# Layer 0's branch and output turned by VectorE's 32x32 block transposes and a trip through memory, in place of TensorE's transposes

## The chip, the core and the metric

One core of a Trainium2 chip runs the whole kernel. The metric is device time of one execution in microseconds (us). TensorE (PE) multiplies, VectorE (DVE) and ScalarE (ACT) work elementwise, GpSimd (POOL) and SyncE (SP) are used here for little else than issuing transfers (DMAs), each from its own queue.

## What is computed

A trunk of two layers over 256 positions of width 2048, all in f32. Layer 0 mixes positions with a gated unit, layer 1 with causal attention. What matters of the reference, shortened:

```python
# layer 0's branch
h = x @ w_in                                  # 2048 -> 3 * 2048
uv = gelu(h[..., :2 * W]); z = h[..., 2 * W:]
u, v = uv[..., :W], layer_norm(uv[..., W:])
s = einsum('gts,bnsgc->bntgc', tril(w_s), v) + b_s
branch = u * s * silu(z)
# both layers, after their branch
y = branch @ w_out[i]
x = layer_norm(ALPHA * x + y)
x = x + sigmoid(x @ w_ple_gate[i]) * (p[i] @ w_ple_proj[i])
```

Layer 1's branch starts with `x @ w_in_b`, whose input is layer 0's `x`.

## The kernel before

**Matmuls.** A matmul contracts over partitions, so its input x or branch must stand with the features on the partitions ("turned"); results come out with positions on the partitions ("rows"). f32 is kept by splitting each operand into a high part (a rounded copy, made by ACT) and a low part (the rest, made by DVE), and adding three products. Rows are handled in four slices `n` of 512 columns and two halves `m` of 128 positions.

**Units.** `row_slice` makes one slice of 512 columns in four `row_unit`s; a unit is 24 matmuls of 128x512 on 1 MB of weights. Layer 0 runs, in this order, the stages v, u, z (the gate: `gated`), y (`after`, w_out), pp, g (`after`, w_gate); then layer 1's v (16 units named y, `row_unit(banks, (2c, 2c+1), ...)`, which use `xs[2c]`, `xs[2c+1]` in order), q/k, attention, z and again `after`.

**Weights.** SP loads each MB in two halves into `wr` (4 buffers, L120), ACT makes `wh` (L121) and DVE `wl` (L122). `wh` and `wl` have 3 buffers, and `weights()` writes the instructions two units ahead. So the load of unit k+3's parts waits until PE has done unit k.

**Order.** `at(units, f)` puts a piece of work behind the given number of units; `tick()`, at each unit's end, writes out what is due. What is written then stands in each engine's queue at about that place, and each engine runs its queue strictly in order. The tile framework gives out buffers of a pool, adds the waits, and may place an instruction that lacks a buffer later in its queue. The pool `r4` (12 buffers of 128x1024 f32) is shared by u, v, gains and biases (`gb`), the rows of x (`R`), their raw form `xq`, and more.

**Turning.** `turn` (L254) takes two 128-column features of both halves: four PE transposes into one PSUM bank `tp` (L260), and `split` (L71) reads the bank for both parts. In layer 0 it turns the branch (8 calls, names u to b) and the output (8 calls, names r to x), each call at the end of the first and second unit after its slice, and the normalised x (8 calls, names r to xn). Layer 1 calls it 8 times more for its own normalised x.

**The residual rows.** x comes in turned, and `R` is made of it without PE: `load_blocks` (L392) reads xT in 32x32 blocks with 64 DMAs on SP (256 runs of 128 bytes each) and `turn_blocks` (L402) transposes each block on DVE. These stand in the z stage, four loads a unit.

Of the kernel before, what the change touches and what calls it, by code (L numbers as in the profile page):

```python
# [8 lines left out]
F32 = mybir.dt.float32  # L9
# [4 lines left out]
P = 128  # L14
D = 2048
S = 256
KT = D // P
NM = S // P
NS = D // 512
# [21 lines left out]
def decoder_trunk(ctx: ExitStack, tc: tile.TileContext, xT, pT, wv_a, wu_a, wz_a, w_sT, b_s,  # L41
# [5 lines left out]
    nc = tc.nc  # L47
# [4 lines left out]
    dram = ctx.enter_context(tc.tile_pool(name="dram", bufs=1, space=bass.MemoryType.DRAM))  # L52
# [8 lines left out]
    def r4(name):  # L61

        return act.tile([P, NM, 512], F32, name=name, tag="r4", bufs=NR4)
# [4 lines left out]
    def in2(t):  # L68
        return t.rearrange("p (i s) -> p i s", i=2)

    def split(src, n="s", g=2):  # L71

        t = t4(n).rearrange("p (g h s) -> p g h s", g=g, h=2)
        src = src.rearrange("p (g s) -> p g s", g=g)
        nc.scalar.activation(t[:, :, 0, :], src, AF.Copy)
        nc.vector.tensor_sub(t[:, :, 1, :], src, f32(t[:, :, 0, :]))
        return t
# [76 lines left out]
    def at(units, f, *args):  # L154

        later.append([units, f, args])
# [97 lines left out]
    def turn(xs, j, rows, n="t"):  # L254
# [7 lines left out]
        t = split(tp, n)  # L262
        xs[2 * j:2 * j + 2] = [t[:, u] for u in range(2)]


    warm = bank("warm")
    for _ in range(WARM):
# [2 lines left out]
    xs = [None] * KT  # L270
# [75 lines left out]
    def spatial(j):  # L346
# [8 lines left out]
        for i in range(2):  # L355
            g = 2 * j + i
            o = us[g // 4][:, :, (g % 4) * P:(g % 4 + 1) * P]
            nc.vector.scalar_tensor_tensor(o, sp[:, i], bsT[:, g:g + 1], o, op0=ALU.add, op1=ALU.mult)

    vgb = [None] * NS  # L360
    at(1, turn_vectors)
    for n in range(NS):
# [10 lines left out]
    def gated(o, xs):  # L373

        br = [None] * KT
        for n in range(NS):
            y = row_slice(xs, "z")
            for m in range(NM):
                t = t2("sz")
                nc.scalar.activation(t, y[m], AF.Silu)  # L380
                nc.vector.tensor_mul(o[n][:, m, :], o[n][:, m, :], t)
            for i in range(2):
                at(1 + i, turn, br, 2 * n + i, o, "b")
        return br


    R = [None] * NS

    x_blocks = xT.rearrange("(f c) k t -> f c k t", f=4)
    xq = [None]  # L390

    def load_blocks(h, m, g):  # L392


        if g == 0:
            xq.append(r4("xq").rearrange("p i s -> p (i s)"))
        t = xq[-1][32 * g:32 * g + 32, :].rearrange("p (k f t) -> p k f t", k=8, f=4)
        c = slice(m * P + 32 * g, m * P + 32 * g + 32)
        for f in range(4):
            nc.sync.dma_start(t[:, :, f, :], x_blocks[f, :, 8 * h:8 * h + 8, c])  # L400

    def turn_blocks(h, m):  # L402
        raw = xq[1 + 2 * h + m]
        for i in range(2):
            if m == 0:
                R[2 * h + i] = r4("r")
            nc.vector.transpose(R[2 * h + i][:, m, :], raw[:, i * 512:(i + 1) * 512])

    for a in range(4):
        for g in range(4):  # L410
            at(1 + 4 * a + g, load_blocks, a // 2, a % 2, g)
        at(6 + 4 * a, turn_blocks, a // 2, a % 2)
    br = gated(us, xs)


    def after(i, br):


        ps_ = t2("pr")
        nc.sync.dma_start(in2(ps_), pT[i])  # L420
        pk = split(ps_, "p")
        st = small.tile([P, NM, NS, 6], F32, name="st")
        mv = small.tile([P, NM, 2], F32, name="mv")
        rs = small.tile([P, NM], F32, name="rs")
        gb = [None] * NS
        for n in range(NS):
            at(2 + 3 * n, lambda n: gb.__setitem__(n, gain_bias(1 + i, n)), n)
        for n in range(NS):
            y = row_slice(br)
            for m in range(NM):  # L430
                r = R[n][:, m, :]
                nc.vector.scalar_tensor_tensor(r, r, ALPHA, y[m], op0=ALU.mult, op1=ALU.add)
                nc.vector.bn_stats(st[:, m, n, :], r)
        for m in range(NM):
            nc.vector.bn_aggr(mv[:, m, :], st[:, m])
        nc.vector.tensor_scalar(rs, mv[:, :, 1], EPS, None, op0=ALU.add)
        nc.gpsimd.tensor_tensor(rs, rs, half, op=ALU.pow)


        pp = []  # L440
        wp = []

        def embed(n, m):
            if m == 0:
                pp.append(r4("pp"))
                if n % 2 == 0:
                    wp[:] = [t.rearrange("p (k n c) -> p k n c", k=2, n=2) for t in weights(1 + n // 2)[2:]]
            ps = bank("pp")
            c = slice(m * P, (m + 1) * P)
            for k in range(2):  # L450
                xh, xl = pk[:, k, 0, c], pk[:, k, 1, c]
                nc.tensor.matmul(ps, xh, wp[0][:, k, n % 2, :], start=k == 0, stop=False)
                nc.tensor.matmul(ps, xl, wp[0][:, k, n % 2, :], start=False, stop=False)
                nc.tensor.matmul(ps, xh, wp[1][:, k, n % 2, :], start=False, stop=k == 1)
            nc.scalar.activation(pp[n][:, m, :], ps, AF.Copy)

        xn = [None] * KT

        def norm_slice(n):
            for m in range(NM):  # L460
                normalise(R[n], gb[n], m, mv[:, m, 0:1], rs[:, m:m + 1])

        units = [(n, m) for n in range(NS) for m in range(NM)]
        for u in units[:5]:
            embed(*u)
        for n in range(2):
            norm_slice(n)
            turn(xn, 2 * n, R, "xn")
            turn(xn, 2 * n + 1, R, "xn")
            if n == 0:  # L470
                for u in units[5:]:
                    embed(*u)

        def rest(n):
            norm_slice(n)
            turn(xn, 2 * n, R, "xn")
            turn(xn, 2 * n + 1, R, "xn")

        at(1, rest, 2)
        at(2, rest, 3)  # L480

        xo = [None] * KT
        for n in range(NS):
            y = row_slice(xn, "g")
            last = i == DEPTH - 1
            for m in range(NM):
                parts = 2 if last and n == NS - 1 else 1
                w = 512 // parts
                t = t2("sg")
                for h in range(parts):  # L490
                    c = slice(h * w, (h + 1) * w)
                    r = R[n][:, m, c]
                    nc.scalar.activation(t[:, c], y[m][:, c], AF.Sigmoid)
                    nc.vector.tensor_mul(t[:, c], t[:, c], pp[n][:, m, c])
                    nc.vector.tensor_add(r, r, t[:, c])
            for h in range(2):
                if not last:
                    at(1 + h, turn, xo, 2 * n + h, R, "x2")
                elif n < NS - 1:
                    at(1 + h, store, 2 * n + h)  # L500
                else:
                    store(2 * n + h)
        return xo
# [15 lines left out]
    xs = after(0, br)  # L519
# [12 lines left out]
    o = [None] * NS  # L532
# [61 lines left out]
    for h in range(KT):  # L594
        t = t2("qk")
# [70 lines left out]
```

## Time and profile before

| | us |
|---|---|
| median of three runs (1053.1 to 1054.34) | 1053.94 |
| the profiled execution | 1053.71 |
| its span, first to last instruction | 1052.0 |
| PE busy in it | 1041.0 (99%) |
| DVE busy | 640.6 (61%) |
| ACT busy | 494.6 (47%) |
| granted TensorE clock, mean | 0.999 |

In rows of the trace, `x24` counts instructions, times are us from the span's start, `[a <-B]` is idle time before a row and what ended it. A timeline merges like instructions that follow each other.

### The profile page before, as it was taken

Reading aid. Unit: us, or ns where it says so; the run is one execution under the profiler, and the core shown is the slowest. Engines: PE = TensorE matmul, PEld = TensorE weight load, DVE = VectorE, ACT = ScalarE, POOL = GpSimd, SP = SyncE. Lnnn points to the kernel's source line nnn. Section 1 sums busy time; section 2 is a strip of 40 time slices with the busy share of each in tenths; the row PEclk is TensorE's granted clock in tenths of the full one; section 3 lists DMA queues with packets and bytes.
Section 4 is the critical chain, followed back from the end, with each engine's and each line's share of the span. In section 5 each row is a group of like instructions: output and inputs, shape, how many; then the busy total and the mean of one; then the engine's idle time right before and its main releaser. Section 6 shows DMA issues by size and latency. Waiting matters only on the chain.

```text
span 1052.0 us, 13393 instructions
## 1 busy us (share of the span) xinstructions
PE 1041.0 (99%) x5136; PEld 876.3 (83%) x5136; DVE 640.6 (61%) x835; ACT 494.6 (47%) x679; POOL 24.6 (2%) x46
## 2 busy tenths in 40 slices
PE   8999999999999999999999999999999999999997
PEld 6888888888888878888888888888888888878886
DVE  5656765565565695555545666666665565568552
ACT  5545453444443364443434555555555453345442
POOL 2100100000000000000000000000000000000000
PEclk9999999999999999999999999999999999999999
DMA  8775664799665545566555555455455555554651
GB/s 265 268 253 183 238 230 167 216 234 228 179 234 200 199 161 200 201 212 208 188 192 192 169 170 170 160 172 170 160 175 186 188 196 190 197 193 167 201 200 40
DMA packets 101232, 203.89 MB, mean 194 GB/s; under 512 B 24192, under 2 KB 26512, under 8 KB 101168
## 3 DMA queue, kind: packets, MB, share of 16 engines
q1 hardware_dynamic: 99152, 196.64, 56.7%
q0 software_dynamic: 2016, 6.40, 2.6%
q8 instruction: 40, 0.66, 0.3%
q14 instruction: 24, 0.20, 0.1%
HBM read 200.86 MB, written 2.15 MB: 193 GB/s over the span
## 4 chain that ended last, share of the span: by engine, by line
issue 57%; PE 40%; DMA 1%; DVE 0%; POOL 0%; ACT 0%; SPq 0%; POOLq 0%; ACTq 0%; DVEq 0%
PE g L204 6%; PE g L206 6%; PE g L208 6%; PE u L206 3%; PE u L208 3%; PE u L204 3%; PE v L206 2%; PE v L208 2%; PE v L204 2%; PE z L206 2%; PE z L208 2%; PE z L204 2%; PE tp L260 1%; DMA wr<-in_wv_a 1%; PE sp L354 1%
## 5 line engine op out<-in xcount | busy, mean ns | idle before, releaser
L122 DVE TENSOR_TENSOR wl<-wr,wh 128x1024 fp32r<-128x1024 f32 (+1 forms) x366 | 432.6, 1203 | 272.2 <-ACT wh L121 267.4
L121 ACT ACTIVATE wh<-wr 128x1024 fp32r<-128x1024 f32 (+1 forms) x366 | 372.1, 1040 | 369.1 <-PE y L206 141.0
L247 PE MATMUL f<-x,wh 128*128 128x512 f32 x768 | 271.0, 396 | 0.0
L247 PE MATMUL f<-x,wl 128*128 128x256 f32 x768 | 206.2, 279 | 0.0
L247 PEld LDWEIGHTS f<-x,wh 128*128 128x128 f32 x768 | 143.2, 188 | 29.9
L247 PEld LDWEIGHTS f<-x,wl 128*128 128x128 f32 x768 | 144.5, 188 | 2.9
L204 PE MATMUL g<-wh,xn 128*128 128x512 f32 x256 | 101.6, 397 | 0.0
L208 PE MATMUL g<-wl,xn 128*128 128x512 f32 x256 | 100.0, 391 | 0.0
L206 PE MATMUL g<-wh,xn 128*128 128x512 f32 x256 | 99.8, 390 | 0.0
L204 PE MATMUL y<-wh,b 128*128 128x512 f32 x256 | 99.8, 390 | 0.0
L208 PE MATMUL y<-wl,b 128*128 128x512 f32 x256 | 99.6, 389 | 0.0
L206 PE MATMUL y<-wh,b 128*128 128x512 f32 x256 | 99.6, 389 | 0.0
L208 PEld LDWEIGHTS g<-wl,xn 128*128 128x128 f32 x256 | 48.0, 188 | 10.2
L208 PEld LDWEIGHTS y<-wl,b 128*128 128x128 f32 x256 | 48.0, 188 | 10.0
L204 PEld LDWEIGHTS y<-wh,b 128*128 128x128 f32 x256 | 48.1, 188 | 10.0
L206 PEld LDWEIGHTS y<-wh,b 128*128 128x128 f32 x256 | 48.1, 188 | 9.9
L206 PEld LDWEIGHTS g<-wh,xn 128*128 128x128 f32 x256 | 48.1, 188 | 9.5
L204 PEld LDWEIGHTS g<-wh,xn 128*128 128x128 f32 x256 | 48.1, 188 | 9.3
L204 PE MATMUL z<-wh,x 128*128 128x512 f32 x128 | 50.4, 394 | 0.0
L204 PE MATMUL u<-wh,x 128*128 128x512 f32 x128 | 49.9, 390 | 0.0
L208 PE MATMUL z<-wl,x 128*128 128x512 f32 x128 | 49.9, 390 | 0.0
L206 PE MATMUL z<-wh,x 128*128 128x512 f32 x128 | 49.9, 390 | 0.0
(142 smaller groups left out, 1236.1 us busy)
## 6 DMA issues: line engine op xcount, KB each, us to landing
wr<-in_wqkz_b SPq DMA_DIRECT2D x96, 512.0 KB, 3.6
wr<-in_w_out SPq DMA_DIRECT2D x64, 512.0 KB, 4.5
wr<-in_w_gate SPq DMA_DIRECT2D x64, 512.0 KB, 4.3
wr<-in_wu_a SPq DMA_DIRECT2D x32, 512.0 KB, 4.3
wr<-in_wz_a SPq DMA_DIRECT2D x32, 512.0 KB, 5.1
wr<-in_wv_b SPq DMA_DIRECT2D x32, 512.0 KB, 4.0
wr<-in_wv_a SPq DMA_DIRECT2D x26, 512.0 KB, 5.2
gb<-vecs POOLq DMA_DIRECT2D x24, 256.0 KB, 6.0
```

What stands on the lines that cost most here:

```text
L121: nc.scalar.activation(hi[:, c], raw, AF.Copy)
L122: nc.vector.tensor_sub(lo[:, c], raw, f32(hi[:, c]))
L204: nc.tensor.matmul(o(n), xh, wh[i][n], start=first, stop=False)
L206: nc.tensor.matmul(o(n), xl, wh[i][n], start=False, stop=False)
L208: nc.tensor.matmul(o(n), xh, wl[i][n], start=False, stop=last)
L247: nc.tensor.matmul(*m, start=k == 0 and j == 0, stop=k == KT - 1 and j == len(ms) - 1, skip_group_check=True)
L260: nc.tensor.transpose(tp[:, u * S + m * P:u * S + (m + 1) * P], rows[f // 4][:, m, (f % 4) * P:(f % 4 + 1) * P], ident)
L354: nc.tensor.matmul(sp[:, i], wt, vt, start=a == 0, stop=a == 2, skip_group_check=True)
```

## The change

A new function `turn_far` turns a whole slice of 512 columns. `block_turn`: DVE transposes the 32x32 blocks of each half into a new tile (two instructions), and POOL's queue writes them to a scratch tensor `d` in memory with eight DMAs, each 32 partitions by 16 runs of 128 bytes, that put every block at its transposed place. `back`, one unit later, reads `d` with two DMAs of 256 KB on POOL's queue. `splits`, four units after the slice, makes both parts of it with two calls of `split`, now from SBUF. `gated` uses it for slices 0 to 2 (the last slice keeps `turn`), `after` for all four slices of layer 0's output. The residual's loads and block transposes move: they are now put on the list ahead of the u stage, 10 to 25 units from there, which is seven units earlier.

```diff
+    def turn_far(xs, n, rows, name):
+        d = dram.tile([512, S], F32, name=f"{name}{n}")
+        t = r4(name + "b")
+
+        def block_turn():
+            for m in range(NM):
+                nc.vector.transpose(t[:, m, :], rows[n][:, m, :])
+            for m in range(NM):
+                for g in range(4):
+                    c = slice(m * P + 32 * g, m * P + 32 * g + 32)
+                    nc.gpsimd.dma_start(d[:, c].rearrange("(b c) t -> c b t", c=32),
+                                        t[32 * g:32 * g + 32, m, :].rearrange("p (b t) -> p b t", t=32))
+
+        def back():
+            raw.append(r4(name + "r"))
+            for j in range(2):
+                nc.gpsimd.dma_start(in2(raw[0][:, j, :]),
+                                    d[j * S:(j + 1) * S, :].rearrange("(u p) t -> p u t", p=P))
+
+        def splits():
+            for j in range(2):
+                s = split(raw[0][:, j, :], name)
+                xs[4 * n + 2 * j:4 * n + 2 * j + 2] = [s[:, u] for u in range(2)]
+
+        raw = []
+        block_turn()
+        at(1, back)
+        at(4, splits)
...
 # gated, after silu and the product of slice n
+            if n < NS - 1:
+                turn_far(br, n, o, "bt")
+                continue
             for i in range(2):
                 at(1 + i, turn, br, 2 * n + i, o, "b")
...
 # load_blocks and turn_blocks stand ahead of the u stage now
-            at(1 + 4 * a + g, load_blocks, a // 2, a % 2, g)
-        at(6 + 4 * a, turn_blocks, a // 2, a % 2)
+            at(10 + 4 * a + g, load_blocks, a // 2, a % 2, g)
+        at(15 + 4 * a, turn_blocks, a // 2, a % 2)
...
 # after, behind slice n of the gate
+            if not last:
+                turn_far(xo, n, R, "xt")
+                continue
             for h in range(2):
-                if not last:
-                    at(1 + h, turn, xo, 2 * n + h, R, "x2")
-                elif n < NS - 1:
+                if n < NS - 1:
```

The queues move at three places. On PE, in the z stage, a unit ahead of which a turn stood (`sp` is layer 0's mixing, `tp` the turn's bank). Before:

```order
L208 MATMUL z<-wl,x 128x512
L354 MATMUL sp<-vs,ws 128x256 x6
L260 MATMUL tp<-ident,u 128x128 x4
L204 MATMUL z<-wh,x 128x512
L206 MATMUL z<-wh,x 128x512
```

and now:

```order
L208 MATMUL z<-wl,x 128x512
L385 MATMUL sp<-vs,ws 128x256 x6
L204 MATMUL z<-wh,x 128x512
L206 MATMUL z<-wh,x 128x512
L208 MATMUL z<-wl,x 128x512
```

Fourteen groups of four transposes are gone from PE's queue in this way, and nothing else in it moves. On ACT, from the silu of z's slice 0 to that of slice 1. Before:

```order
L380 ACTIVATE sz<-z 128x512 [waits PE_49]
L121 ACTIVATE wh<-wr 128x1024 [waits DMAHW7_49,DVE_49,PE_49]
L380 ACTIVATE sz<-z 128x512 [waits PE_49]
L121 ACTIVATE wh<-wr 128x1024 [waits DMAHW0_49]
L121 ACTIVATE wh<-wr 128x1024 [waits DMAHW5_49,DVE_49,PE_49]
L75 ACTIVATE b<-tp 128x2x256 [waits PE_49]
L121 ACTIVATE wh<-wr 128x1024 [waits DMAHW6_49]
L121 ACTIVATE wh<-wr 128x1024 [waits DMAHW3_49,DVE_49,PE_49]
L75 ACTIVATE b<-tp 128x2x256 [waits PE_49]
L121 ACTIVATE wh<-wr 128x1024 [waits DMAHW4_49]
```

and now, from the load of the unit two after the slice (`btr` is what `back` read):

```order
L121 ACTIVATE wh<-wr 128x1024 [waits DMAHW3_49,DVE_49,PE_49]
L121 ACTIVATE wh<-wr 128x1024 [waits DMAHW4_49]
L121 ACTIVATE wh<-wr 128x1024 [waits DMAHW5_49,DVE_49,PE_49]
L121 ACTIVATE wh<-wr 128x1024 [waits DMAHW6_49]
L75 ACTIVATE bt<-btr 128x2x256 [waits DMASW3_49]
L75 ACTIVATE bt<-btr 128x2x256 [waits DMASW4_49]
L438 ACTIVATE sz<-z 128x512 [waits PE_49]
L121 ACTIVATE wh<-wr 128x1024 [waits DMAHW7_49,DVE_49,PE_49]
L438 ACTIVATE sz<-z 128x512 [waits PE_49]
L121 ACTIVATE wh<-wr 128x1024 [waits DMAHW0_49]
```

The splits, which waited for PE inside the next two units' weight loads, now wait for POOL's transfers behind four units' loads and just ahead of the next slice's silu. On SP, in the z stage, where the residual's loads stand among the weights. Before:

```order
L120 DMA wr<-in_wz_a 128x2x512 [waits DMAHW0_49,DVE_49]
L400 DMA xq<-in_xT 32x8x32 [waits DMAHW1_49,DMASW7_49,DMASW0_49]
L400 DMA xq<-in_xT 32x8x32 [waits DMAHW2_49]
L400 DMA xq<-in_xT 32x8x32 [waits DMAHW3_49]
L400 DMA xq<-in_xT 32x8x32 [waits DMAHW4_49]
L120 DMA wr<-in_wz_a 128x2x512 [waits DMAHW5_49,DVE_49]
```

and now, for the last quarter of them:

```order
L120 DMA wr<-in_wz_a 128x2x512 [waits DMAHW4_49,DMAHW0_49,DVE_49]
L404 DMA xq<-in_xT 32x8x32 x4
L404 DMA xq<-in_xT 32x8x32 [waits DMAHW5_49]
L404 DMA xq<-in_xT 32x8x32 [waits DMAHW6_49]
L404 DMA xq<-in_xT 32x8x32 [waits DMAHW7_49]
L404 DMA xq<-in_xT 32x8x32 [waits DMAHW0_49]
```

Eight more `xq` rows, each with the wait for one of the eight semaphores of SP's transfers in turn, follow before the next `wr` row: these sixteen loads stand in one run between the weights of z's units 10 and 11 (counted from 0), where before four stood between the weights of two units. The first three quarters still stand four to a unit, from the u stage's last units on. Each such wait is for the transfer eight places ahead to have landed.

## Rows read from the trace of the kernel before

**Rows 1.** The page: the span, and each engine's busy time and instructions.
```profile
span 1052.0 us, 13393 instructions
PE 1041.0 (99%) x5136; PEld 876.3 (83%) x5136; DVE 640.6 (61%) x835; ACT 494.6 (47%) x679; POOL 24.6 (2%) x46
```

**Rows 2.** Waits of PE, whole span: who waited for whom, us, times, longest.
```profile
PE v L204 <- ACT wh L121: 2.3, 3, 1.3
PE warm L268 <- POOL ident masks.py:199: 1.6, 1, 1.6
PE to L511 <- DVE r L495: 1.4, 1, 1.4
PE tp L260 <- DVE r L329: 1.2, 2, 0.6
```

**Rows 3.** Waits of ACT, the largest: for PE to free a weight buffer.
```profile
ACT wh L121 <- PE y L206: 141.0, 44, 3.4
```

**Rows 4.** Timeline of PE, layer 0's g stage: start, us, instruction.
```profile
403.95 0.39 PE L204 MATMUL g<-wh,xn 128*128 128x512 f32 x1
...
409.39 0.60 PE L260 MATMUL tp<-ident,r 128*128 128x128 f32 x4
...
415.32 0.60 PE L260 MATMUL tp<-ident,r 128*128 128x128 f32 x4
...
432.13 0.60 PE L260 MATMUL tp<-ident,r 128*128 128x128 f32 x4
```

**Rows 5.** The tile tp: duration min/median/max in ns, first and last start.
```profile
L75 ACT ACTIVATE b<-tp x8: 579/598/598, 216.5 to 290.6; 128x512 fp32r<-128x512 f32 x8
...
L75 ACT ACTIVATE x<-tp x8: 579/581/582, 410.3 to 484.2; 128x512 fp32r<-128x512 f32 x8
```

**Rows 6.** Lines of DVE by shape, the residual's block transposes: busy us, mean ns.
```profile
L407 DVE STREAM_TRANSPOSE r<-xq 128x512 f32<-128x512 f32 x8 | 5.3, 690 | 0.0
```

**Rows 7.** Timeline of ACT, z's slice 1, weight loads and what each waited for.
```profile
209.71 1.06 ACT L121 ACTIVATE wh<-wr 128x1024 fp32r<-128x1024 f32 x1 [1.90 <-PE z L206]
...
227.69 2.01 ACT L121 ACTIVATE wh<-wr 128x1024 fp32r<-128x1024 f32 x2 [3.43 <-PE z L206]
...
233.85 2.00 ACT L121 ACTIVATE wh<-wr 128x1024 fp32r<-128x1024 f32 x2
```

**Rows 8.** Timeline of DVE, g's slice 1: a weight part, the product's last sum.
```profile
429.49 1.22 DVE L122 TENSOR_TENSOR wl<-wr,wh 128x1024 fp32r<-128x1024 f32 x1
430.63 0.68 DVE L495 TENSOR_TENSOR r<-r,sg 128x512 f32<-128x512 f32 x1
```

**Rows 9.** Timeline of ACT, g's slice 1: the load that PE's end of slice 1 released.
```profile
426.65 1.06 ACT L121 ACTIVATE wh<-wr 128x1024 fp32r<-128x1024 f32 x1 [1.90 <-PE g L206]
```

**Rows 10.** Lines of POOL by shape, its DMA issues: busy us, mean ns.
```profile
L179 POOL DMA_DIRECT2D gb<-vecs x24 | 13.0, 546 | 233.6 <-DVE sg L494 98.8 <-DMA wr<-in_wz_a 98.4 <-PE tp L260 22.5
...
L172 POOL DMA_DIRECT2D vecs<-tv x1 | 0.6, 567 | 0.8 <-ACT tv L170 0.8
L142 POOL DMA_DIRECT2D bsp<-in_b_s x1 | 0.5, 519 | 0.0
```

**Rows 11.** Line L179, POOL's 256 KB reads: issue in ns, us from issue to landing.
```profile
L179 POOL DMA_DIRECT2D gb<-vecs x24: 536/546/580, 107.0 to 475.9; - x24
...
DMA to landing us min/median/max: 4.6/6.0/7.2
```

**Rows 12.** DMA issues: queue, count, KB each, median us to landing.
```profile
vecs<-tv POOLq DMA_DIRECT2D x1, 48.0 KB, 4.2
```

**Rows 13.** Stretches: us, busy us (instructions) of each engine, clock, DMA share, GB/s.
```profile
133.80:186.50 52.70, 52.70 (x247) 44.13 (x247) 29.88 (x34) 22.84 (x28) 0.00 (x0) 1.00 0.58 195
...
232.60:255.40 22.80, 22.80 (x106) 18.86 (x105) 10.87 (x12) 9.51 (x12) 2.17 (x4) 1.00 1.01 248
```

**Rows 14.** The tile xq, 232.6 to 255.4: issues, and us to landing.
```profile
L400 SPq DMA_DIRECT2D xq<-in_xT x16: 311/456/923, 232.3 to 252.2; - x16
...
DMA to landing us min/median/max: 5.2/6.5/8.1
```

More of the change, by code (lines that the diff above doesn't have):

```diff
@@ L358, in spatial, with load_blocks, turn_blocks @@
             nc.vector.scalar_tensor_tensor(o, sp[:, i], bsT[:, g:g + 1], o, op0=ALU.add, op1=ALU.mult)
+    R = [None] * NS
+    x_blocks = xT.rearrange("(f c) k t -> f c k t", f=4)
+    xq = [None]
+    def load_blocks(h, m, g):
+        if g == 0:
+            xq.append(r4("xq").rearrange("p i s -> p (i s)"))
+        t = xq[-1][32 * g:32 * g + 32, :].rearrange("p (k f t) -> p k f t", k=8, f=4)
+        c = slice(m * P + 32 * g, m * P + 32 * g + 32)
+        for f in range(4):
+            nc.sync.dma_start(t[:, :, f, :], x_blocks[f, :, 8 * h:8 * h + 8, c])
+    def turn_blocks(h, m):
+        raw = xq[1 + 2 * h + m]
+        for i in range(2):
+            if m == 0:
+                R[2 * h + i] = r4("r")
+            nc.vector.transpose(R[2 * h + i][:, m, :], raw[:, i * 512:(i + 1) * 512])
+    for a in range(4):
+        for g in range(4):
+            at(10 + 4 * a + g, load_blocks, a // 2, a % 2, g)
+        at(15 + 4 * a, turn_blocks, a // 2, a % 2)
     vgb = [None] * NS
@@ L384, in gated @@
         return br
[L387 to L410, printed above, removed]
-            at(1 + 4 * a + g, load_blocks, a // 2, a % 2, g)
-        at(6 + 4 * a, turn_blocks, a // 2, a % 2)
     br = gated(us, xs)
```

## The prediction

> **What bounds the kernel now.** I read the page first: PE is busy 1041.0 of 1052.0 us, DVE 61%, ACT 47% [rows 1]. A busy PE is not yet a PE that sets the time, so the waits come next. PE waits seven times in the whole span, 6.5 us together, and none of them is in the stages changed here except 1.2 us at the turns of the normalised x, which stay [rows 2]. The other side agrees: what ACT waits for most is PE, to free a weight buffer [rows 3]. So the weights are always ahead, and whatever PE need not do shortens the time one for one, until something new makes PE wait. The span is 1052.0 us, the profiled execution 1053.71 us, the median 1053.94 us; I take differences in the span as differences of the median.
>
> **What goes: PE's transposes.** The timeline of PE in the g stage gives the price of one turn with everything around it [rows 4]. From 403.95 to 409.39 PE does one unit of 24 matmuls and no turn: 5.44 us. From 409.39 to 415.32 it does a turn and a unit: 5.93 us, so the turn costs 0.49 us. From 415.32 to 432.13 it does a turn and three units: 16.81 us, less 3 x 5.44 is 0.49 us again. That is less than the 0.60 us of the row, since the next matmuls overlap, and more than 4 transposes started back to back, since the first matmuls behind them come slower. The z stage has 8 turns of the branch (u to b) and layer 0's output 8 (r to x) [rows 5]; 6 and 8 go, two stay with the last slice. 14 x 0.49 = **6.9 us**, all on PE's own queue.
>
> The order shows nothing else moved on PE. The splits stay 14 calls; they read SBUF in place of a bank (0.6 us on ACT before [rows 5]; I take the same) and move to a later place in the queue. The freed PSUM banks are worth nothing, since PE waits for no bank [rows 2].
>
> **What comes: DVE.** 14 block transposes of 128x512. The residual has the same instruction at 690 ns [rows 6], so 9.7 us on DVE, 1.4 us a slice in stages where DVE is busy about half the time (10.87 of 22.80 us in z's slice 2) [rows 13]. Hidden: weights are made two units ahead.
>
> **What comes: the trip through memory.** This is where the change can go wrong, because ACT stands still at the splits until the trip is over, with the silu (or sigmoid) of the next slice and the next weights queued behind. So I compare the trip's end with the moment from which PE would feel it. T is PE's end of the slice.
>
> *When PE feels it.* In z's slice 0, T is 209.7. ACT loads the unit that T released, then one more at each unit's end; the load ahead of the splits begins at 227.69 and takes 2.0 us [rows 7]. Less two turns that PE no longer does (1.0 us), ACT reaches the splits at T + 19. Its next load cannot start before T + 22 anyway, when PE ends the next slice; before it began at 233.85 [rows 7]. The weights of that load feed the seventh unit from T, which begins at T + 6 x 5.44, or T + 32.6, and needs its first low part 0.4 us later. From the landing, two splits, a silu, a product, a block transpose and the first half's two parts take an estimated 4.6 us (0.6 us on ACT and 0.7 us on DVE for a 512-wide step [rows 5, 6, 8], 1.06 and 1.22 us for a half's parts [rows 7, 8]). So **a landing up to T + 28.4 costs nothing.** The branch and output themselves are used no earlier: slice 2's at T + 32.6, slice 3 of the output six units after its end.
>
> *When the trip ends.* The later case is g: its last sum ends at 431.31, T being 426.65 [rows 8, 9], so the second block transpose ends at T + 5.4; the first is done by T. In z less stands behind T: a silu, a product and the block transpose, about 2 us. Each half needs four write DMAs on POOL. Their issue price is the unknown: 512 runs of 128 bytes each. POOL's issues took 519 ns for 16 runs, 567 for 96, 546 for 128 [rows 10], hardly more with more runs, so I take 0.6 us; the other end is to scale 546 ns by the runs, 4 x 0.55 = 2.2 us. Below 0.52 us nothing speaks for it. At 0.6 us the last of the eight starts at T + 7.2. The only write from POOL landed 4.2 us after its issue [rows 12], 256 KB reads after 6.0 us (4.6 to 7.2) [rows 11]; writes land by T + 11.4 to 13.2. `back` waits for all eight, then issues two reads 0.55 us apart, the second landing 6.0 us later: **T + 18 to 20**, about when ACT arrives, and 8 us before PE would feel it. At 2.2 us an issue the last write starts at T + 15.6, and the trip ends at T + 26.4 to 28.2; with the longest landing both times, T + 30.6.
>
> Nobody else waits for POOL meanwhile: behind the three branch trips it has the layer norm's gains (`gb`) and the small power, needed some 100 us later, and behind the four output trips the same of layer 1.
>
> *The transfers beside the weights.* A slice adds 4096 runs of 128 bytes and 512 KB of reads. Before, the window 232.6 to 255.4 held sixteen `xq` loads, 4096 runs of 128 bytes too, and four `gb` reads, 1 MB [rows 14, 13]. There the DMA share was 1.01, against 0.58 in 133.8 to 186.5, and PE did not wait. So a slice with a trip is a load that the weights have stood already. These are reads, though; no row shows a write in runs of 128 bytes.
>
> **What moves: the residual's loads.** The same 64 DMAs and 8 block transposes. Three quarters stand four to a unit as before. The last sixteen stand in one run on SP, and the weights of z's unit 11 behind them. Each waits for the transfer eight places ahead, so two landings of 6.5 us [rows 14] and the issues make about 10 us of SP. The weights behind would otherwise go out some 5 us later than the run begins, so they are 5 to 6 us late, against about 11 us from a weight's usual issue to the moment PE misses it: no cost, with some 5 us left.
>
> **Sum.** 1053.94 - 6.9 + 0 = **1047.1 us**. The forecast's own range is 1046.3 to 1048.0, about a tenth of the turns' price either way.
>
> **Rivals.**
> 1. *The trip outlasts its cover* (slower). If POOL's issue goes with the runs, and landings are the longest seen, the trip ends at T + 30.6, 2.2 us too late, in each of seven slices: 1047.1 + 15.4 = 1062.5 us. It costs nothing up to 2.2 us an issue with usual landings, and from 1 us a slice beyond T + 28.4 the gain is gone. For it: POOL is never seen with so many runs. Against: 16 to 128 runs differ by under 50 ns, and all 24 `gb` issues took 536 to 580 ns [rows 11] while DVE worked about half the time [rows 13].
>    The Trainium skill, page SBUF — State Buffer, section Who interferes with whom, has a rule against the change: GpSimd and VectorE share a port pair, so that a VectorE instruction with two SBUF inputs, as the low parts are, holds up a GpSimd instruction that reads SBUF, and one in a two-port mode keeps GpSimd from writing a transfer's descriptors. Were every issue to sit out one such instruction, 1.22 us [rows 8], it would be 1.8 us, and by the working above still in time; by the rows on the 24 issues no such hold shows, and I leave the chance where they put it.
> 2. *The run of sixteen residual loads.* With landings of 8.1 us, the longest in that window [rows 14], SP is held for about 14 us; DVE, whose queue has the last block transposes of the residual ahead of unit 11's weights, waits until about 23 us after the run began, and PE then some 2 to 4 us, once: 1049 to 1051 us. For it: the trip of slice 1 falls into the same time. Against: the median landing leaves 5 us.
> 3. *Writes in short runs hold the DMA engines.* The window of slice 2 shows (1.01 - 0.58) x 22.8 = 9.8 us of engine time for 4096 read runs and 1 MB [rows 13]; some 7 of it may be the runs. The weights take 0.58 x 22.8 = 13.2 us of a slice and the 512 KB read back perhaps 2, so it decides from about 7.6 us for the runs. If writing costs twice those 7, the slice needs 29 us in place of 22.8: 6 us late, seven times, 1047 + 43 = 1090 us. For it: no row shows such writes. Against: as many reads left PE without a wait.
>    The Trainium skill, page DMA: Bandwidth & Descriptors, section Specifications, says that transfers under 512 bytes are done as a read, a change and a write; by that the runs could well cost twice, and the time would be this rival's. No row here shows it for writes.
> 4. *Nothing is gained*, because the weights turn out to set the pace as soon as PE is quicker: 1053.9 us. Against it are rows 3: in the y units ACT waited for PE 44 times, 3.2 us each.
>
> **Chances.** Forecast 0.72; rival 1 0.09; rival 2 0.10; rival 3 0.05; rival 4 0.04. The forecast and rival 2 together hold 0.82, so the range is 1046.0 to 1051.0. About 0.2% (2.1 us) is what a measurement here can tell from no change, so faster means below 1051.8. Faster: 0.72 and most of rival 2, 0.80. Within 0.2%: rival 4, the rest of rival 2, a little of rival 1, 0.07. Slower: rivals 1 and 3, 0.13.
>
> **What would show it.** In the changed kernel's trace: 5.44 us from unit to unit through z, g and layer 1's v, with no gap where the turns stood; PE's waits still near 6.5 us. POOL's write issues at 0.6 us; landings of the second read near T + 20, with ACT's idle time before `bt<-btr` and `xt<-xtr` ended by DMA and at most a few us. The prediction is wrong if PE waits for `wh` or `wl` in z, g or the first units of layer 1's v: with ACT held at the splits it is rival 1, with SP held at `xq` rival 2, with weights landing late everywhere rival 3.

## The result, and the profile after

The changed kernel takes 1046.97 us (median of six runs, 1046.09 to 1048.48); the kernel before took 1053.99 us beside it (six runs). The ratio is 0.9934, with a 95% interval of 0.9923 to 0.9945: 7.0 us less. The prediction was 1047.1 us.

The page of the changed kernel: span, engines, and the queue of POOL's transfers (packets, MB, share of 16 engines):

```profile
span 1046.8 us, 13390 instructions
...
PE 1035.7 (99%) x5080; PEld 872.0 (83%) x5080; DVE 650.3 (62%) x849; ACT 496.0 (47%) x679; POOL 70.2 (7%) x116
...
q0 software_dynamic: 4928, 13.74, 4.7%
```

PE has 56 instructions less than in [rows 1], which are the 14 turns of four, and is busy 5.3 us less. POOL, which did next to nothing, has 70 instructions more. All waits of PE in the whole span (who waited for whom, us, times, longest):

```profile
PE v L204 <- ACT wh L121: 2.3, 3, 1.1
PE warm L299 <- POOL ident masks.py:199: 1.6, 1, 1.6
PE to L546 <- DVE r L529: 1.4, 1, 1.4
PE tp L260 <- DVE r L360: 1.2, 2, 0.6
```

These are the seven waits of [rows 2], 6.5 us again, at the same four places. No new wait has come, so what PE no longer does is gained in full. The timeline of PE shows where. Its first matmul of the u stage, the first of the output stage `y`, the first of the g stage's long run behind its last turn, and the first of layer 1's `v` (named y, on the `xt` that came through memory):

```profile
97.02 0.39 PE L204 MATMUL u<-wh,x 128*128 128x512 f32 x1
...
277.30 0.39 PE L204 MATMUL y<-wh,bt 128*128 128x512 f32 x1
...
391.61 0.48 PE L204 MATMUL g<-wh,xn 128*128 128x512 f32 x1
...
467.90 0.62 PE L204 MATMUL y<-wh,xt 128*128 128x512 f32 x2
```

From 391.61 to 467.90 stand 14 units without a break: 76.29 / 14 = 5.45 us a unit, the 5.44 us that [rows 4] gave for a unit with no turn.

The start of the kernel, ahead of u's first matmul, takes 94.9 to 98.1 us in the profiles below. Every engine runs the same instructions in the same order there in all twelve kernels, so this scatter comes from no edit, and I compare kernels from u's first matmul. A row of the table is one execution, the profiled one; only its last column is the median of all. In it, *u* and *y* are the starts of the first matmul of u and of the output stage, read as above from each trace:

| kernel | u | y | span | u to y | u to end | median time |
|---|---|---|---|---|---|---|
| before | 95.48 | 278.62 | 1052.0 | 183.1 | 956.5 | 1053.99 |
| after | 97.02 | 277.30 | 1046.8 | 180.3 | 949.8 | 1046.97 |
| branch alone | 95.71 | 275.99 | 1049.7 | 180.3 | 954.0 | 1051.50 |
| output alone | 96.04 | 279.21 | 1048.7 | 183.2 | 952.7 | 1050.36 |
| writes in 4 | 95.39 | 282.73 | 1074.1 | 187.3 | 978.7 | 1078.79 |
| writes in 8 | 95.74 | 276.70 | 1136.6 | 181.0 | 1040.9 | 1139.33 |
| writes on SP | 95.94 | 286.30 | 1068.6 | 190.4 | 972.7 | 1069.12 |
| residual's loads late | 96.72 | 281.24 | 1055.2 | 184.5 | 958.5 | 1057.02 |
| the same, splits at 5 | 98.14 | 278.70 | 1053.6 | 180.6 | 955.5 | 1050.08 |
| last slice too | 94.92 | 275.19 | 1043.9 | 180.3 | 949.0 | 1046.10 |
| layer 1's output too | 95.46 | 275.74 | 1042.6 | 180.3 | 947.1 | 1044.50 |
| both | 95.34 | 275.62 | 1041.6 | 180.3 | 946.3 | 1044.02 |

After against before: 2.9 us less from u to y (six turns, 0.48 us each), and 6.7 us from u to the end (14 turns, 0.48 us each). The 0.3 us that are left of the 7.0 are within the scatter of single executions.

The trips come out close to the prediction's working. POOL's issues by line: duration min/median/max in ns, first and last start; then, by line, us from issue to landing (writes, then reads):

```profile
L277 POOL DMA_DIRECT2D xt<-xtb x32: 648/651/709, 403.6 to 475.8; - x32
L277 POOL DMA_DIRECT2D bt<-btb x24: 648/649/682, 211.1 to 263.4; - x24
...
DMA to landing us min/median/max: 2.3/4.2/6.4
...
L283 POOL DMA_DIRECT2D xtr<-xt x8: 713/718/730, 415.5 to 483.3; - x8
L283 POOL DMA_DIRECT2D btr<-bt x6: 716/718/722, 221.8 to 270.0; - x6
...
DMA to landing us min/median/max: 4.9/5.5/7.0
```

By the transfers' landings the second read of a trip ended at T + 17.8, 21.3 and 21.5 us in z and at T + 19.1, 19.7, 20.7 and 20.6 us in g, T being PE's end of the slice. ACT had to wait for them a little, 8.0 us in eight waits:

```profile
ACT bt L75 <- DMA btr<-bt: 4.4, 4, 1.3
ACT xt L75 <- DMA xtr<-xt: 3.6, 4, 1.8
```

and DVE's block transposes took 0.71 us each, 10.0 us in all:

```profile
L273 DVE STREAM_TRANSPOSE xtb<-r 128x512 f32<-128x512 f32 x8 | 5.7, 711 | 0.3
...
L273 DVE STREAM_TRANSPOSE btb<-u 128x512 f32<-128x512 f32 x6 | 4.3, 709 | 0.1
```

### The profile page after: what moved, and what is told of

The parts are those of the page before. It is cut to its first block, busy times and chain, and to the rows that moved or that the text cites. A ratio compares the mean times of both kernels' runs of the same rounds, so it can differ in the third digit from the quotient of the medians.

```text
span 1046.8 us, 13390 instructions
## 1 busy us (share of the span) xinstructions
PE 1035.7 (99%) x5080; PEld 872.0 (83%) x5080; DVE 650.3 (62%) x849; ACT 496.0 (47%) x679; POOL 70.2 (7%) x116
## 4 chain that ended last, share of the span: by engine, by line
issue 53%; PE 36%; DMA 7%; DVE 2%; POOL 1%; ACT 1%; POOLq 0%; SPq 0%; ACTq 0%; DVEq 0%
PE g L206 4%; PE g L204 4%; PE g L208 4%; PE u L206 3%; PE u L204 3%; PE u L208 3%; PE z L204 2%; PE v L206 2%; PE z L208 2%; PE v L208 2%; PE z L206 2%; PE v L204 2%; DMA xt<-xtb 2%; DMA wr<-in_wv_a 2%; DMA xtr<-xt 2%
## 5 line engine op out<-in xcount | busy, mean ns | idle before, releaser
L247 PE MATMUL f<-xt,wh 128*128 128x512 f32 x768 | 271.0, 396 | 0.0
L247 PE MATMUL f<-xt,wl 128*128 128x256 f32 x768 | 206.2, 279 | 0.0
L247 PEld LDWEIGHTS f<-xt,wh 128*128 128x128 f32 x768 | 143.2, 188 | 29.9
L247 PEld LDWEIGHTS f<-xt,wl 128*128 128x128 f32 x768 | 144.5, 188 | 2.9
L204 PE MATMUL y<-wh,b 128*128 128x512 f32 x160 | 62.2, 389 | 0.0
L206 PE MATMUL y<-wh,b 128*128 128x512 f32 x160 | 62.2, 389 | 0.0
L208 PE MATMUL y<-wl,b 128*128 128x512 f32 x160 | 62.2, 389 | 0.0
L208 PEld LDWEIGHTS g<-wl,xn 128*128 128x128 f32 x256 | 48.1, 188 | 10.1
L204 PE MATMUL u<-wh,x 128*128 128x512 f32 x128 | 49.9, 390 | 0.0
L206 PE MATMUL u<-wh,x 128*128 128x512 f32 x128 | 49.9, 390 | 0.0
L208 PE MATMUL u<-wl,x 128*128 128x512 f32 x128 | 49.8, 389 | 0.0
L204 PE MATMUL v<-wh,x 128*128 128x512 f32 x128 | 38.7, 399 | 2.3 <-ACT wh L121 2.3
```

Source lines behind the costliest of these rows:

```text
L204: nc.tensor.matmul(o(n), xh, wh[i][n], start=first, stop=False)
L206: nc.tensor.matmul(o(n), xl, wh[i][n], start=False, stop=False)
L208: nc.tensor.matmul(o(n), xh, wl[i][n], start=False, stop=last)
L247: nc.tensor.matmul(*m, start=k == 0 and j == 0, stop=k == KT - 1 and j == len(ms) - 1, skip_group_check=True)
```

## The experiments

**One half at a time.** The whole change less its part in `after`, then less its part in `gated` (the early loads of the residual stay in both):

```diff
-            if not last:
-                turn_far(xo, n, R, "xt")
-                continue
             for h in range(2):
-                if n < NS - 1:
+                if not last:
+                    at(1 + h, turn, xo, 2 * n + h, R, "x2")
+                elif n < NS - 1:
```

```diff
-            if n < NS - 1:
-                turn_far(br, n, o, "bt")
-                continue
```

> Only the branch's slices 0 to 2 take the trip through memory; layer 0's output is turned by PE again, 8 turns. The residual's loads stay at their new place. Theory (PE no longer does the turns, and no wait takes their place): 6 turns x 0.49 us are gone, so 2.9 us less than the kernel before, and from the u stage's first matmul to the y stage's first 180.3 us as in the changed kernel (183.1 before). Rival (the moved residual loads bring the gain): about 7 us less than before, as with the whole change.

> Only layer 0's output takes the trip; the branch is turned by PE again, 8 turns. The residual's loads stay at their new place. Theory: 8 turns x 0.49 us are gone, so 3.9 us less than the kernel before; together with the branch alone (2.9 us) this is the whole change's 6.8 to 7 us. Rival (the moved loads bring the gain): about 7 us less here too. Rival (the trips of the two places hinder each other or the weights): the two parts sum to more than the whole.

Measured: the branch alone 1051.50 us (ratio to before 0.9978, 0.9969 to 0.9987), the output alone 1050.36 us (0.9965, 0.9954 to 0.9977). From u to the end, 2.5 and 3.9 us less than before; the whole change 6.7. The branch alone gained its full 2.9 us by the first y and lost 0.4 us in the output stage, in the one execution looked at. The sum, 6.4 us, is 0.3 us from the whole; by the medians it is 2.2 + 3.3 = 5.5 of 7.0 us, with an interval of about 1 us either way on each half. Both halves contain the early loads of the residual. These gain nothing by themselves: with the output alone, where the loads are early and the branch takes no trip, it is 183.2 us from u to y, and 183.1 before.

**How much later may a trip be?** Each write is cut, in four DMAs of 128 runs or eight of 64, with the bytes and the places the same. The first of the two:

```diff
-                    nc.gpsimd.dma_start(d[:, c].rearrange("(b c) t -> c b t", c=32),
-                                        t[32 * g:32 * g + 32, m, :].rearrange("p (b t) -> p b t", t=32))
+                    for q in range(4):
+                        nc.gpsimd.dma_start(
+                            d[128 * q:128 * (q + 1), c].rearrange("(b c) t -> c b t", c=32),
+                            t[32 * g:32 * g + 32, m, 128 * q:128 * (q + 1)].rearrange("p (b t) -> p b t", t=32))
```

> The whole change, but each write of a trip is cut into four DMAs of 128 runs: the same bytes and runs, 32 issues a slice in place of 8. PE's queue reads as in the whole change. Theory (an issue costs POOL much the same whatever its runs, 0.55 to 0.6 us for 128 runs, against 0.65 us read for 512): a slice's issues take 18 us in place of 5.2, the second read lands at about T + 30 to T + 33 in place of T + 18 to 21.5, past the T + 28.4 up to which the prediction found that a landing costs nothing. So PE should wait for weights, 2 to 5 us in each of seven slices: 1047.0 + 14 to 35 = 1061 to 1082 us. Rival a (the issue's price goes with the runs, 0.16 us for 128): the trip ends where it did, 1047 us. Rival b (the issues do cost 18 us, but the cover is longer than the prediction's T + 28.4): POOL's issues at 0.55 us, ACT waits about 10 us a slice for the reads, PE does not, 1047 us.

> Each write of a trip cut into eight DMAs of 64 runs, 64 issues a slice. Theory: 64 x 0.55 = 35 us of POOL a slice, more than the 21.8 us of a slice, so the trips queue behind each other: the second read lands near T + 47, the next ones later still. The framework now places splits and units of the output stage in another order, which takes back a part. At least 10 us late in most of seven slices: 1100 us or more, and PE waits for weights (ACT held at the splits) in z and g. Rival a (the price goes with the runs, 0.08 us each): 1047 us. Rival b (the longer cover together with the new order hides all): below 1055 us.

Measured: 1078.79 us (1.0244, 1.0228 to 1.0259) and 1139.33 us (1.0804, 1.0782 to 1.0826). POOL's issues, of 128 runs in the first and of 64 in the second:

```profile
L278 POOL DMA_DIRECT2D bt<-btb x96: 551/552/575, 209.5 to 281.6; - x96
```

```profile
L278 POOL DMA_DIRECT2D bt<-btb x192: 533/542/566, 209.8 to 329.7; - x192
```

An issue costs 0.54 us for 64 runs, 0.55 for 128 and 0.65 for 512: a fixed price with hardly anything for the runs. That settles the prediction's unknown: the price does not go with the runs. With 32 issues a slice the trips are late, and the size of the cover can be read. ACT, writes in four, at the splits of z's slice 0:

```profile
235.51 0.63 ACT L75 ACTIVATE bt<-btr 128x512 fp32r<-128x512 f32 x1 [5.28 <-DMA btr<-bt]
237.83 0.63 ACT L75 ACTIVATE bt<-btr 128x512 fp32r<-128x512 f32 x1 [1.68 <-DMA btr<-bt]
```

By its timeline PE ended that slice at 209.64, and the trip landed at 237.80, T + 28.2. PE did not wait. The next trip landed at 265.98, T + 33.8 with T at 232.14, and there PE waited, for weights whose ACT loads stood behind the splits:

```profile
264.57 0.39 PE L208 MATMUL z<-wl,x 128*128 128x512 f32 x1
268.19 0.79 PE L204 MATMUL z<-wh,x 128*128 128x512 f32 x1 [3.23 <-ACT wh L121]
...
269.84 0.80 PE L208 MATMUL z<-wl,x 128*128 128x512 f32 x1 [0.43 <-DVE wl L122]
```

The unit that waits is the seventh from T, due 0.23 us behind the first of these rows, at T + 32.7: the place that the prediction named. It began 3.4 us late. Its first low part, due 0.45 us behind its start, came at 269.84, 4.6 us late, where a cover to T + 28.4 gives 33.8 - 28.4 = 5.4 us. So in z the cover ends between T + 28.2 and about 33.8 - 4.6, T + 29.2.

The table has more for this kernel than these waits: 7.0 us more from u to y than in the changed kernel, and 28.9 us more to the end, where PE's new waits are 18.5 us. Behind the wait PE's clock was at the lower of its two levels (1.2 of 2.4 GHz, the 0.50 below), and matmuls started 0.43 us apart in place of 0.23:

```profile
269.80:274.60 4.80, 4.76 (x11) 3.80 (x12) 4.02 (x4) 1.29 (x2) 4.64 (x9) 0.50 0.87 262
```

(The columns of such a row: stretch, us, busy us of PE, PEld, DVE, ACT, POOL, granted clock, DMA share, GB/s.) And not every trip ends in a wait of this kind. The longest one is at a place that the prediction did not name, the last slice's turn, which PE still does: it needs a product whose silu stands on ACT behind the third trip's splits.

```profile
297.63 0.90 PE L260 MATMUL tp<-ident,u 128*128 128x128 f32 x3 [9.19 <-DVE u L441]
```

Two more waits, 5.4 us together, are in layer 1's v. In the kernel with 64 issues the trips queue up behind each other until the stage that uses them waits for the splits themselves:

```profile
PE y L204 <- ACT xt L75: 41.1, 3, 25.3
PE y L204 <- ACT bt L75: 27.6, 2, 14.7
```

**The residual's loads at their old place.** They stand in the z stage again, four loads to a unit:

```diff
-    for a in range(4):
-        for g in range(4):
-            at(10 + 4 * a + g, load_blocks, a // 2, a % 2, g)
-        at(15 + 4 * a, turn_blocks, a // 2, a % 2)
 ...
+    for a in range(4):
+        for g in range(4):
+            at(1 + 4 * a + g, load_blocks, a // 2, a % 2, g)
+        at(6 + 4 * a, turn_blocks, a // 2, a % 2)
     br = gated(us, xs)
```

> The whole change, with the residual's loads and block transposes left where they were before (in the z stage, four loads to a unit, no run of sixteen on SP). Theory: moving them gained nothing and cost nothing, the same time as the whole change within 0.3 us, PE's waits alike; only ACT's wait of 5.9 us for a weight load behind the run of sixteen is gone, and one or two others take its place, since the loads now fall into the same units as two of the trips. Rival (moving them is what made room for the trips on the DMA engines): the trips of z's slices 1 and 2 land 3 us or more later, PE waits in the z stage or at the start of the output stage, 2 to 8 us slower, 1049 to 1055.

Measured: 1057.02 us (1.003, 1.0019 to 1.0042), 10 us more than the whole change and slower than before. The theory fell. The rival got the size wrong too, and its cause: counted from u's first matmul, the trips of z's slices 1 and 2 land 2.2 and 1.5 us later than in the changed kernel, not 3 us (the last at 278.16, there at 276.98). What differs most is where ACT comes to its splits. The changed kernel, ACT's timeline ahead of the output stage:

```profile
271.83 2.01 ACT L121 ACTIVATE wh<-wr 128x1024 fp32r<-128x1024 f32 x2 [3.43 <-PE z L206]
275.13 0.63 ACT L75 ACTIVATE bt<-btr 128x512 fp32r<-128x512 f32 x1 [1.29 <-DMA btr<-bt]
```

and with the loads late:

```profile
267.29 1.06 ACT L121 ACTIVATE wh<-wr 128x1024 fp32r<-128x1024 f32 x1 [2.64 <-DMA wr<-in_wz_a]
277.27 0.63 ACT L75 ACTIVATE bt<-btr 128x512 fp32r<-128x512 f32 x1 [8.93 <-DMA btr<-bt]
278.19 0.63 ACT L75 ACTIVATE bt<-btr 128x512 fp32r<-128x512 f32 x1 [0.28 <-DMA btr<-bt]
278.72 1.04 ACT L121 ACTIVATE wh<-wr 128x1024 fp32r<-128x1024 f32 x1
...
280.15 1.04 ACT L121 ACTIVATE wh<-wr 128x1024 fp32r<-128x1024 f32 x1
```

The framework put the third trip's splits one unit's weights earlier into ACT's queue. ACT stands there 8.9 us, and the two loads behind, at 278.72 and 280.15, are the weights of the output stage's first unit. PE:

```profile
281.24 0.50 PE L204 MATMUL y<-wh,bt 128*128 128x512 f32 x1 [3.53 <-ACT wh L121]
```

PE was done with z at 277.6 and begins y at 281.24. After the wait its clock is not whole either (0.50 from 283.8 to 285.9, and as a mean of a longer stretch):

```profile
277.00:299.00 22.00, 16.42 (x66) 12.20 (x65) 13.54 (x16) 11.61 (x16) 1.08 (x2) 0.92 0.68 224
```

In the changed kernel the stretch 270 to 299 has a granted clock of 1.00 and PE does not wait in it.

Was it the place in ACT's queue, or did the late loads crowd out the weights? The same kernel, with the branch's splits put on the list one unit later, which moves the third trip's alone, to behind the weights of the output stage's second unit:

```diff
-    def turn_far(xs, n, rows, name):
+    def turn_far(xs, n, rows, name, due=4):
...
-        at(4, splits)
+        at(due, splits)
...
-                turn_far(br, n, o, "bt")
+                turn_far(br, n, o, "bt", 5)
```

> The residual's loads late, as in e6, but the branch's splits are put on the list five units after their slice instead of four. The framework keeps the first two trips' splits where e6 has them and moves the third's: in e6 they stand on ACT ahead of the weights of the output stage's first unit, here behind those of its second unit and ahead of the last slice's turned branch. All DMAs and PE's queue stay as in e6. Theory (e6 lost its time because ACT, held 8.9 us at the third trip's splits, made the weights behind them late; the transfers themselves were not the trouble): the 4.2 us that e6 lost ahead of the output stage's first matmul are back, most of what it lost in that stage's first units too; from u's first matmul to the end about 950 to 953 us in place of e6's 958.5, 1047 to 1050 us. Rival (the late loads crowd the DMA engines, and weights come late by that): like e6, 1055 to 1058 us.

Measured: 1050.08 us (0.9969, 0.9958 to 0.9980), 6.9 of the 10 us back. The 4.2 us ahead of y's first matmul are gone, 180.6 us from u to y. Some 3 us are left. The profiled execution took 1055.37 us, the longest of its eleven, so its rows show the place and not the usual size; there all that is lost against the changed kernel, but for 0.3 us, lies in the output stage:

```profile
289.38 0.63 ACT L75 ACTIVATE p<-pr 128x512 fp32r<-128x512 f32 x1 [7.90 <-DMA pr<-in_pT]
```

ACT is held there by the load of the small input `pr`, with weights queued behind, and PE waits 3.3 us for them at 293.96. The changed kernel has the same wait of ACT (8.3 us) and no wait of PE behind it; there ACT has the splits behind it by then, and here they stand between `p` and the next weights. So most of the 10 us is shown to be the place of the splits; what the rest comes from was not tried.

**The writes on SP's queue.**

```diff
-                    nc.gpsimd.dma_start(d[:, c].rearrange("(b c) t -> c b t", c=32),
+                    nc.sync.dma_start(d[:, c].rearrange("(b c) t -> c b t", c=32),
```

> The whole change, but the trip's writes are issued from SP's queue, among the weights, in place of POOL's. The framework now counts on a shorter trip and puts the splits on ACT only two weight loads after the silu, in place of eight, about T + 8. Theory: SP's issues are cheaper than POOL's 0.65 us, but a write waits in SP's queue for DVE's block transpose and the weights stand behind it, and the trip cannot end before the writes' 4 us and the reads' 5.5 us are over, T + 14 or later; ACT is held 5 us or more in most slices with weights queued behind, and PE waits 1 to 5 us a slice: 1052 to 1080 us. Rival (the shorter issues bring the trip in by more than SP's queue loses): 1047 us or a little less, no PE wait in z and g.

Measured: 1069.12 us (1.014, 1.0125 to 1.0154). The same writes on SP and their landing; then ACT's wait in z and the output stage, and PE's waits:

```profile
L277 SPq DMA_DIRECT2D bt<-btb x24: 302/500/511, 209.8 to 269.8; - x24
...
DMA to landing us min/median/max: 1.8/2.0/3.6
```

```profile
ACT bt L75 <- DMA btr<-bt: 14.3, 3, 10.2
```

```profile
PE g L204 <- ACT wh L121: 8.8, 2, 6.7
PE z L204 <- ACT wh L121: 4.6, 2, 3.9
```

A write is cheaper and lands twice as soon from there, and the kernel is 22 us slower than the changed one. Two causes show. The splits stand two weight loads behind the silu in place of eight, ahead of weights that PE soon needs, and ACT stands at them for up to 10.2 us. And the next weights stand behind the writes on SP, which wait for DVE's block transposes. So it is at PE's longest wait, the 6.7 us at 476.49; SP's queue ahead of it, and then ACT:

```profile
456.01 9.72 SPq L277 DMA_DIRECT2D xt<-xtb  x8
465.83 1.99 SPq L120 DMA_DIRECT2D wr<-in_w_gate  x4
```

```profile
470.35 1.06 ACT L121 ACTIVATE wh<-wr 128x1024 fp32r<-128x1024 f32 x1 [9.97 <-DMA wr<-in_w_gate]
```

How the 22 us divide between the two was not tried. Faster transfers gained nothing here.

**The branch's last slice too.** Its splits are put on the list after three units, since layer 0's output stage begins there:

```diff
-            if n < NS - 1:
-                turn_far(br, n, o, "bt")
-                continue
-            for i in range(2):
-                at(1 + i, turn, br, 2 * n + i, o, "b")
+            turn_far(br, n, o, "bt", 4 if n < NS - 1 else 3)
```

> The branch's last slice takes the trip too, its splits written three units after the slice, since the y stage's fourth unit uses them. Two more turns leave PE, 1.0 us. Theory (a trip costs nothing only while it ends before its cover does): the trip ends 18 to 21.5 us after the slice, two splits and a low part later its first piece is there at 20 to 23 us, and PE wants it after three units, 16.3 us; PE waits 4 to 7 us once in the y stage, and the kernel is 3 to 6 us slower than the whole change, about 1 to 4 us faster than the kernel before. Rival (the cover is no matter, since PE runs behind what the trace shows): 1.0 us faster than the whole change.

Measured: 1046.10 us (0.9928, 0.9913 to 0.9943); from u to the end 949.0 us, 0.8 less than the whole change. My theory fell. The time is near its rival's, but not for the rival's reason. The framework moved the next slice's first unit, which uses slices that are long there, ahead of the first slice's fourth on PE. So the trip landed at 291.54, 16.4 us after the z stage, as PE began the unit that had been moved ahead (291.51), and nobody waited; ACT reached the splits after it:

```profile
291.48 2.01 ACT L121 ACTIVATE wh<-wr 128x1024 fp32r<-128x1024 f32 x2 [3.43 <-PE y L206]
293.40 1.13 ACT L75 ACTIVATE bt<-btr 128x512 fp32r<-128x512 f32 x2
```

**Layer 1's output too.** Its slices 0 to 2 are block-transposed and written by POOL straight to the output, which is turned as well:

```diff
+    def out_far(n):
+        t = r4("ob")
+        for m in range(NM):
+            nc.vector.transpose(t[:, m, :], R[n][:, m, :])
+        d = out[512 * n:512 * (n + 1), :]
...
+            if n < NS - 1:
+                out_far(n)
+                continue
             for h in range(2):
```

> The whole change, and layer 1's output too: slices 0 to 2 are turned by DVE's blocks and written by POOL straight to the output, 8 write DMAs a slice; nothing reads them back. Six more turns (the line with the tile to) leave PE, and ACT's copies of them. Theory: 6 x 0.49 = 2.9 us less than the whole change, 9.8 us less than the kernel before, near 1044.1 us. Rival (the end of the kernel is set by the last writes, or the weights near the end cannot go faster): no gain over the whole change.

Measured: 1044.50 us (0.9913, 0.9899 to 0.9928). From u to the end 2.6 us less than the whole change, for six turns: 0.44 us each.

**Both.**

> The whole change, and also the branch's last slice by the trip (e3) and layer 1's output slices 0 to 2 block-transposed and written by POOL to their place in the output (e7). Both left out PE turns of their own: 2 and 6 more. By the differences read from first matmul of u to the end, e3 gained 0.8 us over the whole change and e7 2.6 us: together 946.4 us from there, and with a start of 95 to 97 us a span of 1041.4 to 1043.4, a time of 1043.1 to 1045.1 us. Rival (the gains do not add, since the units which the framework moves ahead in e3 are no longer free): the time of e7 alone, 1044.5 us, or more.

Measured: 1044.02 us (0.9906, 0.9893 to 0.9920), 946.3 us from u to the end, as worked out: the gains add up. PE's waits are at the four places of before. The writes to the output, issue in ns and landing:

```profile
L547 POOL DMA_DIRECT2D out<-ob x24: 651/651/705, 970.6 to 1019.9; - x24
...
DMA to landing us min/median/max: 2.3/2.7/5.9
```

It is faster than both kernels, by 9.8 us than the kernel before (1053.86 us beside it) and by 3 us than the change.

## Why the prediction was right, point by point

The mechanism is the one that was forecast. That the time agrees to 0.1 us is in part luck: from u to the end the profiles differ by 6.7 us, where 6.9 were forecast, and single executions of the changed kernel lie up to 2.4 us apart.

**PE bounds the kernel, one for one.** Right. 22 turns are gone in the last kernel, 14 in the changed one, 8 and 6 in its halves, and each time u to the end shrank by 0.42 to 0.48 us a turn, with the waits of [rows 2] unchanged. Rival 4, weights that set the pace, is out.

**0.49 us a turn.** 0.48 measured. The row of a turn alone, 0.60 us [rows 4], would have given 8.4 us, and the 0.35 us from its first transpose to the next matmul's start 4.9; the difference between a unit with and without a turn was the one to take.

**DVE hidden.** Right in effect: 14 block transposes of 0.71 us, against the 0.69 of [rows 6], and no wait of PE came of them.

**The trip's end.** T + 18 to 20 predicted, T + 17.8 to 21.5 read. The issue is the 0.6 us taken (0.65), not the 2.2 us at the other end; the reads landed after 5.5 us for the 6.0 of [rows 11]; the writes after 4.2, as the one row there was [rows 12]. The prediction took g for the later case, but the latest trips are two of z, at T + 21 and later. Their second half was written late: its first write was issued 4.1 and 3.5 us after the first half's, 2.7 in the other one, since it waits for a product and a block transpose that stand behind weights on DVE. In the later of the two the first half was late as well, its first write at T + 2.6 (T - 0.2 and T + 0.9 in the others): the silu stood on ACT behind the splits of the trip before, which landed just then. So a late trip makes the next one later.

**The cover.** About right in size, T + 28.2 to 29.2 in z by the cut writes for the T + 28.4 worked out. One step of that working is wrong: it asks for the parts of the first half of the unit's weights only, but a matmul there reads columns of both halves, and in the kernel with writes in four the waiting unit began (268.19) and got its low part (269.84) only when the second half's parts were done (268.14 and 269.79).

Rival 1's size is out by the issue price, but its mechanism is real, and the cut writes show it, at the predicted place and at others. By the Trainium skill, page SBUF — State Buffer, section Who interferes with whom, a VectorE instruction in a two-port mode would keep POOL from writing its descriptors, and one with two SBUF inputs would hold up a POOL instruction that reads SBUF. With DVE busy 62%, mostly with differences of two SBUF tiles of 1.22 us [rows 8], the 56 write issues ran from 648 to 709 ns, so no hold of that length shows here.

**The transfers beside the weights.** Right, with room. In g, the first of two slices before, and the same two after (columns as above, the last but one is the DMA share):

```profile
403.90:426.70 22.80, 22.80 (x106) 18.83 (x106) 13.23 (x14) 10.13 (x13) 1.12 (x2) 1.00 0.63 209
```

```profile
402.50:424.30 21.80, 21.80 (x98) 18.06 (x97) 14.03 (x17) 10.19 (x12) 6.65 (x10) 1.00 0.76 238
424.30:446.00 21.70, 21.70 (x98) 17.96 (x97) 14.31 (x17) 10.28 (x12) 6.59 (x10) 1.00 0.77 243
```

Before, the slice from 426.7 had 0.62. The share grew by 0.76 x 21.8 - 0.63 x 22.8 = 2.2 us of all DMA engines, 2.6 by the second pair. But each slice before also held two reads of `gb`, 1.9 us (8.3% of 45.5 us for two slices on POOL's queue), which come later in the changed kernel. So a trip is 4.1 to 4.5 us there; the transfers of POOL's queue alone took 17.3% of 43.5 us in the two slices after, 3.8 us a trip, and over all seven trips 3.1 us by the pages (4.7% of the span, 2.6% before). The prediction allowed about 9 (7 for the runs and 2 for the read), and rival 3 needed more than 7.6 for the runs alone. By the Trainium skill, page DMA: Bandwidth & Descriptors, section Specifications, transfers under 512 bytes are done as a read, a change and a write; whatever is done, 4096 writes of 128 bytes with their read back did not cost more than these 4.5 us.

**The residual's loads.** Right for the changed kernel. The run of sixteen held SP for 10.1 us (10 predicted), ACT then waited 5.9 us for weights (5 to 6 predicted), and PE did not:

```profile
226.77 10.12 SPq L404 DMA_DIRECT2D xq<-in_xT  x16
```

```profile
242.19 1.06 ACT L121 ACTIVATE wh<-wr 128x1024 fp32r<-128x1024 f32 x1 [5.94 <-DMA wr<-in_wz_a]
```

But the prediction costed the move only as a risk, rival 2, and did not see what it is worth: without it, and with the splits where `at(4, ...)` puts them, the trips cost more than they bring, 1057.0 us. The cover of 8 us that it counted on was that of the order as it stood. How far ahead of the weights the splits stand belongs to the cover, and an edit elsewhere in the queues can take a unit, 5.4 us, from it.

## What to carry to other kernels

Where one engine is busy nearly all the time and waits for nothing, work moved off it is gained at the price of the difference between a stretch with it and one without, even where the way round takes 20 us and four engines. What decides is the instruction that waits for the way round: note which in-order queue it stands in, what stands behind it, and when the bound engine needs that. Look at the order again after every edit, for a scheduler can move just that instruction, as the framework did here with the splits.

## What was not expected of the hardware

- An issue on POOL costs 0.54 to 0.65 us for 64 to 512 runs of 128 bytes; few DMAs with many runs are the cheap form. The same write of 512 runs from SP's queue took 0.50 us and landed after 2.0 us in place of 4.2.
- 4096 written runs of 128 bytes, with 512 KB read back, cost 3.1 to 4.5 us of all DMA engines.
- A wait of PE cost more than its length here: with 5.8 us of new waits in the kernel with late loads, u to the end grew by 8.7 us over the changed kernel, with 15.3 us in the one with writes on SP by 22.9, and with 18.5 us in the one with writes in four by 28.9. The granted clock was 0.50 for 2 to 5 us behind such waits (283.8 to 285.9, 269.8 to 274.6).
